# Scale columns by a product with ones, shift sums queued behind the scale sums, and transposes four steps later

## The chip, the cores and the metric

The kernel runs on one core of a Trainium2 chip. A core has a tensor engine (TensorE, PE in the profile; PEld is its loading of weights), a vector engine (VectorE, DVE), a scalar engine (ScalarE, ACT), GpSimd (POOL) and SyncE (SP), on which most transfers are issued. Each engine works through its own list of instructions in a fixed order and waits where an operand or a buffer isn't ready. The metric is the device time of one execution in microseconds (us), the median of several runs.

## The reference

One layer of a hybrid decoder block on a sequence of S = 512 tokens with D = 2048 channels, all in float32. A vector c sets six modulation vectors; the first norm's output is scaled by one and shifted by another; one wide input projection (7168 columns) feeds eight heads of dilated window attention and eight heads of a gated linear recurrence (HGRN2); then an output projection, a second modulated norm and a squared-ReLU MLP. What matters for this change is the head of it:

```
mod = silu(c) @ w_ada + b_ada                    # 2048 -> 6 * 2048
shift1, scale1, gate1, shift2, scale2, gate2 = split(mod, 6)
h = rms_norm(x, norm1_w) * (1 + scale1) + shift1
proj = h @ w_in                                  # 512 x 2048 by 2048 x 7168
aq, ak, av, gq, gf, gi, gg = split(proj)         # gq at 3072, gf at 4096, gi at 5120
```

## The kernel before

**Splitting.** A float32 product is made from three products of rounded parts: a matrix is cast to a high part (`whi`, `hi`; ScalarE) and VectorE subtracts it to get the low part (`wlo`, `lo`); hi·hi, hi·lo and lo·hi are summed. A weight block of 128 x 512 so costs one ScalarE cast (L39), one VectorE subtraction (L40) and three times as many matmuls. The pool `wr` keeps four blocks of each kind, so a new `whi` waits until TensorE has read the one four before it.

**Scale and shift as sums on VectorE.** A product of a vector with a matrix is done by `gemv` (L113 to L131): rows of the matrix come by DMA into `araw`, and VectorE adds, row group by row group, `araw * vec[k]` into two sums `acc` (L127 the first two, L129 the others). What remains is a sum over the 128 partitions. `to_cols` (L138 to L152) does it: four TensorE transposes of 128 x 128 (L149), then ScalarE copies with an accumulated row sum (L152), which leaves the result as a column per 128 channels. `mod_cols` (L160 to L170) adds the bias (L167) and, for the scale, forms `(1 + scale) * norm weight` (L169), both on VectorE. The scale is made in eight blocks of 256 columns, each enough for two channel tiles; the shift in four blocks of 512.

**First stage, scale only.** `x` is normalised and transposed to sixteen tiles `xnT` (128 channels x 512 tokens). `first_groups(4096, 3072, ...)` then runs over the sixteen channel tiles k, in pairs: `scale_block(k0)` makes the scale block of that pair and calls `scaled(k)`: ScalarE multiplies `xnT` by the column `g1c` (L332), casts it to `hi` (L333), and VectorE forms `lo` (L334). Per k there are 18 matmuls of 128 x 512 (L206 to L208): twelve for gf's first 512 columns (banks `prj`) and six for gq's first 256 (`prc`). The shift is left out here and added to the results afterwards.

**Second stage.** After k0 = 14, `shift_start` starts the shift: `bgw` is a list of generators, and every `bg_step()` runs one of them to its next `yield`. The same loops run again for the next columns with `shift_block` after each pair; once a shift block is done, `shifted(k)` adds the column `s1c` to `xnT` and renews `hi` and `lo` (L337 to L339). 

**Third stage.** `shift_through(col0)` gives the contribution of the shift to the first stage's columns: a `gemv` with `s1c` over w_in's columns (16 steps), `to_cols` (1 step later the transposes), then the gates (`forget`) or the SiLU (L748 to L751). One for columns 4096 and one for 3072 run during the end of the second stage and during `hv0`, the projection of gi (columns 5120), which has twelve matmuls per k (L198 to L200) and makes two background steps per k. What is left of `bgw` after `hv0` is run at once by `while bgw: bg_step()`, ahead of `q0`, the next projection. Then come k, v, the recurrence, the attention, the output projection and the MLP.

**What sets the order.** Through the second stage a scheduler orders each engine's list by estimated times; `tc.issue_after(x)` forbids an instruction ahead of x. From `hv0` on, TensorE's list follows the order in which the code is written, while the other engines' lists are still ordered by the scheduler.

Of the kernel before, what the change touches and what calls it, by code (L numbers as in the profile page):

```python
# [44 lines left out]
def hybrid_block(ctx, tc, x, c, positions, norm1_w, w_ada, b_ada, w_in, q_norm_w, k_norm_w,  # L45
# [3 lines left out]
    pe, dve, act, pool = nc.tensor, nc.vector, nc.scalar, nc.gpsimd  # L49
# [3 lines left out]
    ada_v = w_ada[0].rearrange("(k p) n -> p k n", p=P)  # L53
# [14 lines left out]
    def bank(name, tag="bg"):  # L68
        return ps.tile([P, 512], F32, name=name, tag=tag)


    ident = const.tile([P, P], F32, name="ident")
    make_identity(nc, ident)
    mhalf = const.tile([P, 32], F32, name="mhalf")
    pool.memset(mhalf, -0.5)

    crow = ca.tile([P, P], F32, name="crow", tag="rows")
    nc.sync.dma_start(crow[0:NK], c[0].rearrange("(r p) -> r p", p=P))
# [4 lines left out]
    n1c = const.tile([P, NK], F32, name="n1c")  # L83
    dve.tensor_copy(n1c, ps_c[:, NK:2 * NK])
    bcol = const.tile([P, 96], F32, name="bcol")
    dve.tensor_copy(bcol, ps_c[:, 2 * NK:P])
    sc = const.tile([P, NK], F32, name="sc")
    sig_ready = act.activation(sc, ps_c[:, 0:NK], AF.Sigmoid)
    sc_ready = dve.tensor_tensor(sc, ps_c[:, 0:NK], sc, op=ALU.mult)
# [26 lines left out]
    def gemv(view, vec, col0, n=512, early=False):  # L116

        accs = [(work("acc") if early else gv.tile([P, 512], F32, name="acc"))[:, 0:n] for _ in range(2)]
        nk = 512 // n
        for k0 in range(0, NK, nk):  # L120
            raw = spare.pop(0) if early and spare else slot("araw") if early else gv.tile([P, 512], F32, name="araw", bufs=4)
            raw = raw.rearrange("p (k n) -> p k n", n=n)
            nc.sync.dma_start(raw, view[:, k0:k0 + nk, col0:col0 + n])
            for k in range(k0, k0 + nk):
                acc = accs[k % 2]
                if k < 2:
                    dve.tensor_scalar(acc, raw[:, k - k0], vec[:, k:k + 1], None, op0=ALU.mult)  # L127
                else:
                    dve.scalar_tensor_tensor(acc, raw[:, k - k0], vec[:, k:k + 1], acc, op0=ALU.mult, op1=ALU.add)  # L129
            yield  # L130
        gemv.acc = accs  # L131

    def run_all(g):
        for _ in g:
            pass
        return gemv.acc

    def to_cols(accs, dst):  # L138

        nb = accs[0].shape[1] // P  # L140
        parts = 1 if nb == 4 else 2
        if parts == 1:
            dve.tensor_tensor(accs[0], accs[0], accs[1], op=ALU.add)
        yield
        pc = bank("pc")
        for j in range(nb):
            for u in range(parts):
                c = (j * parts + u) * P
                pe.transpose(pc[:, c:c + P], accs[u][:, j * P:(j + 1) * P], ident)  # L149
        for j in range(nb):  # L150
            c = pc[:, j * parts * P:(j + 1) * parts * P]
            act.activation(c, c, AF.Copy, accum_out=dst[:, j:j + 1])  # L152

    g1c = const.tile([P, NK], F32, name="g1c")
    s1c = const.tile([P, NK], F32, name="s1c")
# [1 line left out]
    s2c = const.tile([P, NK], F32, name="s2c")  # L157
    gcol = const.tile([P, NK], F32, name="gcol")

    def mod_cols(kind, b, dst, nw, n=512, early=False):  # L160

        for _ in gemv(ada_v, sc, kind * D + b * n, n, early):
            yield
        nb = n // P
        d = dst[:, b * nb:(b + 1) * nb]
        yield from to_cols(gemv.acc, d)
        dve.tensor_tensor(d, d, bcol[:, kind * NK + b * nb:kind * NK + (b + 1) * nb], op=ALU.add)  # L167
        if nw is not None:
            mod_cols.last = dve.scalar_tensor_tensor(d, d, 1.0, nw[:, b * nb:(b + 1) * nb], op0=ALU.add, op1=ALU.mult)  # L169
        yield  # L170

    def mod_rows(kind, dst):
# [53 lines left out]
    def slot(name, dt=F32):  # L226
        return io.tile([P, 512], dt, name=name, tag="io")

    def work(name, dt=F32):
        return wk.tile([P, 512], dt, name=name, tag="wk")  # L230

    def pair(i):

        return [hp.tile([P, S], F32R, name=f"{c}{i}", tag=f"{c}{i}") for c in ("hi", "lo")]
# [7 lines left out]
    hhi, hlo, spare = [], [], []  # L242


    first_scale = mod_cols(1, 0, g1c, n1c, 256, True)
    for _ in range(8):
        next(first_scale)
    xs = [[slot("xs") for _ in range(4)] for _ in range(NT)]
# [5 lines left out]
    for q in range(4):  # L254
        for ti in range(NT):
            jk = work("jk")
            with tc.issue_after(sc_ready.ins), tc.issue_after(sig_ready.ins):
                if q == 3 and ti % 2:
                    dve.tensor_tensor_reduce(jk, xs[ti][q], xs[ti][q], op0=ALU.mult, op1=ALU.add, scale=1.0, scalar=0.0,
                                             accum_out=ssx[:, ti, q:q + 1])  # L260
# [2 lines left out]
    dve.tensor_reduce(rx, ssx, axis=AX.X, op=ALU.add)  # L263
    rstd_of(rx, rx, NT, 1.0 / D)
    run_all(first_scale)
    second_scale = mod_cols(1, 1, g1c, n1c, 256, True)
    spare.extend(hp.tile([P, 512], F32, name="araw", tag=f"{c}{k}") for k in range(8, NK) for c in ("hi", "lo"))
    for _ in range(8):
        next(second_scale)
    xnT = []  # L270
# [29 lines left out]
    def scale_block(k0):  # L300
        if k0 == 0:
            run_all(second_scale)
        elif k0 < 14:
            run_all(mod_cols(1, k0 // 2 + 1, g1c, n1c, 256, True))
        for k in (k0, k0 + 1):
            scaled(k)

    def shift_start(k0):
        if k0 == 14:
            for _ in range(12):  # L310
                bg_step()

    shift_done, behind = set(), []

    def shift_gen(b):
        yield from mod_cols(0, b, s1c, None, 512, True)
        shift_done.add(b)

    def shift_block(k0):
# [9 lines left out]
    def scaled(k):  # L329
        for l, t in zip((hhi, hlo), pair(k)):  # L330
            l.append(t)
        act.activation(xnT[k], xnT[k], AF.Copy, scale=g1c[:, k:k + 1])  # L332
        act.copy(hhi[k], xnT[k])  # L333
        dve.tensor_tensor(hlo[k], xnT[k], hhi[k].bitcast(F32), op=ALU.subtract)  # L334

    def shifted(k):
# [404 lines left out]
    def shift_through(col0):  # L741

        yield from gemv(win_v, s1c, col0, early=col0 < 4096 + 512)
        col = sm.tile([P, 8], F32, name="scol", bufs=2)
        yield from to_cols(gemv.acc, col[:, 0:4])
        for h in range(4):
            if col0 == 3072:
                dve.tensor_scalar(col[:, 4 + h:5 + h], col[:, h:h + 1], QS, None, op0=ALU.mult)  # L748
                sg = wk.tile([P, 512], F32, name="sg", tag="ev", bufs=2)
                act.activation(sg, hq0[h], AF.Sigmoid, scale=1.0 / QS, bias=col[:, h:h + 1])  # L750
                dve.scalar_tensor_tensor(hq0[h], hq0[h], col[:, 4 + h:5 + h], sg, op0=ALU.add, op1=ALU.mult)  # L751
            else:
# [5 lines left out]
    bt, bc = first_groups(4096, 3072, scale_block, shift_start)  # L758
    f0 = keep(bt, "f")
    hq0 = keep(bc, "gq", QS)  # L760
    with tc.issue_after(mod_cols.last.ins):
        posf = ca.tile([NT, P], F32, name="posf")
        dve.tensor_copy(posf, posi)
        ps_v = bank("ps_v")
# [615 lines left out]
```

## Time and profile before

| | |
|---|---|
| median of 3 runs | 2312.09 us (2311.49 to 2312.19) |
| profiled execution | 2306.17 us |
| its span, first to last instruction | 2304.4 us |
| TensorE busy | 2230.5 us (97 %) |
| VectorE busy | 1825.9 us (79 %) |
| ScalarE busy | 1103.0 us (48 %) |
| mean granted TensorE clock | 0.994 |

Busy time is the union of an engine's instructions; matmuls overlap in the records, one of 128 x 512 lasting about 0.39 us and the next starting 0.227 us behind it. In the timeline a row stands for a run of like instructions, and a number in brackets at its end is the time in which the engine stood idle ahead of it, with the instruction that released it. Numbers behind names of buffers are left out in the profile; in the engines' lists below they are kept, since each `acc` there is one sum.

### The profile page before, as it was taken

To read this page: it belongs to the slowest core of one execution; us is meant where nothing else is said; L and a number is where in the kernel's file an instruction comes from. 1 tells how busy PE (TensorE), PEld (TensorE's weight loads), DVE (VectorE), ACT (ScalarE), POOL (GpSimd) and SP (SyncE) were. 2 spreads that over 40 slices of the span, in tenths; PEclk is the share of its full clock that TensorE was granted. 3 is DMA by queue.
4 is the path that set the end of the run, shared out by engine and by line. 5 is a ranking of instruction groups with operands and counts; after the bars stand their busy time and mean duration, and the time that the engine had idled before them with its cause. 6 is when DMAs were issued, how large, how long until landed. Compare 5 with 4: busy or idle time off the path is not lost.

```text
span 2304.4 us, 33163 instructions
## 1 busy us (share of the span) xinstructions
PE 2230.5 (97%) x11769; PEld 1829.2 (79%) x11769; DVE 1825.9 (79%) x2773; ACT 1103.0 (48%) x1958; POOL 458.1 (20%) x668
## 2 busy tenths in 40 slices
PE   4999999999999999999999999999998999999999
PEld 3787877888778888888887888888887888888887
DVE  6899777677776565669767988988895789967878
ACT  5555434433344553457644555565563333344332
POOL 1000022000230000001332323323232222222221
PEclk9999999999999999999999999999999999999999
DMA  9798455556545256746999799889889987999784
GB/s 327 249 337 314 123 176 156 176 162 215 178 149 182 74 186 218 259 132 220 366 382 382 252 341 355 301 297 380 310 295 369 339 288 262 364 336 335 277 302 165
DMA packets 264695, 606.71 MB, mean 263 GB/s; under 512 B 23284, under 2 KB 44032, under 8 KB 264528
## 3 DMA queue, kind: packets, MB, share of 16 engines
q1 hardware_dynamic: 186800, 332.54, 42.8%
q0 software_dynamic: 72832, 262.60, 31.1%
q10 hardware_dynamic: 4896, 9.44, 1.2%
q8 instruction: 93, 1.52, 0.3%
q14 instruction: 74, 0.61, 0.1%
HBM read 522.68 MB, written 81.81 MB: 262 GB/s over the span
## 4 chain that ended last, share of the span: by engine, by line
PE 56%; DMA 16%; DVE 14%; issue 10%; POOL 2%; ACT 1%; SPq 0%; DVEq 0%; POOLq 0%; ACTq 0%
PE f L1160 9%; PE f L1161 9%; PE f L1159 9%; DMA araw<-in_w_ada_dram 7%; PE prj L198 4%; PE prj L200 4%; PE prj L199 4%; DMA f_lod<-fs 3%; DVE acc L129 3%; PE f L208 2%; PE f L206 2%; PE f L207 2%; DVE vlo L1146 2%; DVE wlo L40 2%; PE prj L206 2%
## 5 line engine op out<-in xcount | busy, mean ns | idle before, releaser
L1145 ACT CAST vhi<-raw 128x1024 fp32r<-128x1024 f32 x392 | 412.8, 1055 | 547.1 <-PE f L1161 434.3
L1146 DVE TENSOR_TENSOR vlo<-raw,vhi 128x1024 fp32r<-128x1024 f32 x392 | 477.4, 1225 | 154.3 <-ACT vhi L1145 153.5
L1159 PE MATMUL f<-vhi,Fh 128*128 128x512 f32 x1376 | 537.6, 391 | 8.3 <-DMA Fh<-h_hid 3.6
L1160 PE MATMUL f<-vlo,Fh 128*128 128x512 f32 x1376 | 538.1, 391 | 3.0 <-DVE vlo L1146 3.0
L1161 PE MATMUL f<-vhi,Fl 128*128 128x512 f32 x1376 | 537.2, 390 | 2.1 <-DMA Fl<-f_lod 1.3
L39 ACT CAST whi<-wraw 128x512 fp32r<-128x512 f32 (+1 forms) x368 | 219.8, 601 | 449.3 <-PE prj L200 323.7
L198 PE MATMUL prj<-whi,hi 128*128 128x512 f32 x896 | 365.0, 407 | 1.3 <-ACT gg L698 1.3
L200 PE MATMUL prj<-whi,lo 128*128 128x512 f32 x896 | 351.5, 392 | 0.0
L199 PE MATMUL prj<-wlo,hi 128*128 128x512 f32 x896 | 350.8, 391 | 0.0
L40 DVE TENSOR_TENSOR wlo<-wraw,whi 128x512 fp32r<-128x512 f32 (+1 forms) x368 | 245.1, 670 | 111.7 <-ACT whi L39 107.1
L129 DVE SCALAR_TENSOR_TENSOR acc<-araw,sc,acc 128x512 f32<-128x512 f32 (+1 forms) x392 | 253.9, 678 | 98.5 <-DMA araw<-in_w_ada_dram 97.2
L1159 PEld LDWEIGHTS f<-vhi,Fh 128*128 128x128 f32 x1376 | 259.0, 188 | 63.3 <-issue 7.1
L1160 PEld LDWEIGHTS f<-vlo,Fh 128*128 128x128 f32 x1376 | 259.0, 188 | 61.7 <-DVE vlo L1146 8.3
L1161 PEld LDWEIGHTS f<-vhi,Fl 128*128 128x128 f32 x1376 | 259.1, 188 | 56.7 <-DMA Fl<-f_lod 1.8
L1129 DVE TENSOR_TENSOR raw<-raw,raw 128x1024 f32<-128x1024 f32 x224 | 269.5, 1223 | 1.8 <-DMA raw<-in_w_ff_dram 1.5
L198 PEld LDWEIGHTS prj<-whi,hi 128*128 128x128 f32 x896 | 169.4, 189 | 36.5 <-ACT gg L698 1.6
L200 PEld LDWEIGHTS prj<-whi,lo 128*128 128x128 f32 x896 | 168.9, 188 | 36.8
L199 PEld LDWEIGHTS prj<-wlo,hi 128*128 128x128 f32 x896 | 169.6, 189 | 32.4 <-DVE wlo L40 0.4
L1097 POOL DMA_DIRECT2D Fh<-f_hid x112 | 80.9, 722 | 428.3 <-PE f L1161 414.8
L208 PE MATMUL f<-hi,wlo 128*128 128x512 f32 x256 | 99.8, 390 | 0.6 <-DVE wlo L40 0.6
L206 PE MATMUL f<-hi,whi 128*128 128x512 f32 x256 | 100.2, 391 | 0.0
L207 PE MATMUL f<-lo,whi 128*128 128x512 f32 x256 | 99.6, 389 | 0.0
(306 smaller groups left out, 2956.9 us busy)
## 6 DMA issues: line engine op xcount, KB each, us to landing
raw<-in_w_ff_dram SPq DMA_DIRECT2D x224, 512.0 KB, 10.0
araw<-in_w_ada_dram SPq DMA_DIRECT2D x384, 256.0 KB, 4.3
Fh<-f_hid POOLq DMA_DIRECT2D x112, 512.0 KB, 6.5
Fl<-f_lod POOLq DMA_DIRECT2D x112, 512.0 KB, 7.4
wraw<-in_w_in_dram SPq DMA_DIRECT2D x104, 512.0 KB, 4.1
Fh<-h_hid POOLq DMA_DIRECT2D x60, 512.0 KB, 6.8
Fl<-h_lod POOLq DMA_DIRECT2D x60, 512.0 KB, 8.3
f_hid<-part POOLq DMA_DIRECT2D x48, 512.0 KB, 8.1
```

The lines of the kernel that those rows point to most:

```text
L39: nc.scalar.copy(hi, src)
L40: (eng or nc.vector).tensor_tensor(lo, src, hi.bitcast(F32), op=ALU.subtract)
L129: dve.scalar_tensor_tensor(acc, raw[:, k - k0], vec[:, k:k + 1], acc, op0=ALU.mult, op1=ALU.add)
L198: pe.matmul(banks[ti], lhsT=hi[:, ts], rhs=whi, start=first, stop=False)
L199: pe.matmul(banks[ti], lhsT=hi[:, ts], rhs=wlo, start=False, stop=False)
L200: pe.matmul(banks[ti], lhsT=lo[:, ts], rhs=whi, start=False, stop=last)
L1129: dve.tensor_tensor(dst, a, b, op=ALU.subtract)
L1145: act.copy(hi, src)
L1146: split_done.append(dve.tensor_tensor(lo, src, hi.bitcast(F32), op=ALU.subtract))
L1159: pe.matmul(banks[t], lhsT=fh[u][:, a, ts], rhs=whi[:, a], start=first, stop=False)
L1160: pe.matmul(banks[t], lhsT=fh[u][:, a, ts], rhs=wlo[:, a], start=False, stop=False)
L1161: pe.matmul(banks[t], lhsT=fl[u][:, a, ts], rhs=whi[:, a], start=False, stop=end)
```

## The change

There are five edits.

1. Scale blocks get a function of their own, `scale_cols`. The sum over partitions is a float32 product of the sum's 128 x 128 part (as weights) with a column of ones, four products per block in place of four transposes; the two sums `acc` are added in PSUM. ScalarE then forms the scale column from it in one instruction per column, with norm weight as scale and `(1 + bias) * norm weight` as bias (`b1c`, made once at the start); L152 and the two VectorE instructions L167 and L169 go for these blocks.
2. `scaled(k)` writes `hi` from `xnT` and `g1c` directly, ahead of the scaling of `xnT`.
3. The first twelve background steps, the start of the shift's sums, are held behind the last VectorE instruction of the last scale block; the tables for the rotary embedding behind that too.
4. `to_cols` gets a parameter `lag`, the number of background steps between the last sum and its transposes; `shift_through` passes 5 in place of 1.
5. `to_cols` and `mod_cols` lose the 256-column case.

```diff
+    pool.memset(mhalf[:, 16:32], 1.0)
+    ones = mhalf[:, 16:17]
...
+    b1c = bcol[:, NK:2 * NK]
+    dve.scalar_tensor_tensor(b1c, b1c, 1.0, n1c, op0=ALU.add, op1=ALU.mult)
...
+    def to_cols(accs, dst, lag=1):
+
+        dve.tensor_tensor(accs[0], accs[0], accs[1], op=ALU.add)
+        for _ in range(lag):
+            yield
         pc = bank("pc")
...
+    def scale_cols(b):
+
+        for _ in gemv(ada_v, sc, D + b * 256, 256, True):
             yield
+        accs = gemv.acc
+        scale_cols.last_dve = gemv.last
+        pc = bank("pc")
+        for j in range(2):
+            for u in range(2):
+                pe.matmul(pc[:, j:j + 1], lhsT=accs[u][:, j * P:(j + 1) * P], rhs=ones, start=u == 0, stop=u == 1)
+        for j in range(2):
+            ks = slice(2 * b + j, 2 * b + j + 1)
+            scale_cols.last = act.activation(g1c[:, ks], pc[:, j:j + 1], AF.Identity, scale=n1c[:, ks],
+                                             bias=b1c[:, ks])
+        yield
...
         if k0 == 14:
-            for _ in range(12):
-                bg_step()
+            with tc.issue_after(scale_cols.last_dve.ins):
+                for _ in range(12):
+                    bg_step()
...
+        act.activation(hhi[k], xnT[k], AF.Copy, scale=g1c[:, k:k + 1])
         act.activation(xnT[k], xnT[k], AF.Copy, scale=g1c[:, k:k + 1])
-        act.copy(hhi[k], xnT[k])
...
-        yield from to_cols(gemv.acc, col[:, 0:4])
+        yield from to_cols(gemv.acc, col[:, 0:4], 5)
...
-    with tc.issue_after(mod_cols.last.ins):
+    with tc.issue_after(scale_cols.last.ins), tc.issue_after(scale_cols.last_dve.ins):
```

VectorE's list near the end of the first stage, before: `acc_967` and `acc_968` are the sums of the scale block for k = 12 and 13, `acc_1076` and `acc_1077` those of the last block, `acc_1251` and `acc_1252` the first shift block; `g1c` is the scale column.

```order
L127 TENSOR_SCALAR acc_1251<-araw_1253,sc_86 128x512
L129 SCALAR_TENSOR_TENSOR acc_967<-araw_997,sc_86,acc_967 128x256
L129 SCALAR_TENSOR_TENSOR acc_1076<-araw_1090,sc_86,acc_1076 128x256
L127 TENSOR_SCALAR acc_1252<-araw_1256,sc_86 128x512
L167 TENSOR_TENSOR g1c_111<-g1c_111,bcol_84 128x2
L129 SCALAR_TENSOR_TENSOR acc_1077<-araw_1090,sc_86,acc_1077 128x256
L129 SCALAR_TENSOR_TENSOR acc_968<-araw_997,sc_86,acc_968 128x256
L40 TENSOR_TENSOR wlo_1027<-wraw_1020,whi_1026 128x512
L40 TENSOR_TENSOR wlo_1033<-wraw_1030,whi_1032 128x256
L129 SCALAR_TENSOR_TENSOR acc_1251<-araw_1259,sc_86,acc_1251 128x512
L129 SCALAR_TENSOR_TENSOR acc_1076<-araw_1094,sc_86,acc_1076 128x256
L129 SCALAR_TENSOR_TENSOR acc_1252<-araw_1262,sc_86,acc_1252 128x512
```

The same place now, where `acc_1064` and `acc_1065` are the last scale block and `acc_1237` and `acc_1238` the first shift block:

```order
L40 TENSOR_TENSOR wlo_1025<-wraw_1018,whi_1024 128x256
L133 SCALAR_TENSOR_TENSOR acc_1064<-araw_1086,sc_88,acc_1064 128x256
L133 SCALAR_TENSOR_TENSOR acc_1065<-araw_1086,sc_88,acc_1065 128x256
L133 SCALAR_TENSOR_TENSOR acc_1064<-araw_1090,sc_88,acc_1064 128x256
L133 SCALAR_TENSOR_TENSOR acc_1065<-araw_1090,sc_88,acc_1065 128x256
L133 SCALAR_TENSOR_TENSOR acc_1064<-araw_1094,sc_88,acc_1064 128x256
L133 SCALAR_TENSOR_TENSOR acc_1065<-araw_1094,sc_88,acc_1065 128x256
L131 TENSOR_SCALAR acc_1237<-araw_1239,sc_88 128x512
L131 TENSOR_SCALAR acc_1238<-araw_1242,sc_88 128x512
L782 CAST posf_1287<-posi_93 4x128
L353 TENSOR_TENSOR lo12_1106<-xnT_429,hi12_1105 128x512
```

The shift's sums have moved from among the scale's to behind their end, and the two small instructions on `g1c` (L167, and L169 a row later) are gone.

TensorE's list in `hv0`, at the transposes of the first `shift_through`: before,

```order
L200 MATMUL prj_2103<-whi_2244,lo6_793 128x512
L149 MATMUL pc_2266<-ident_69,acc_2058 128x128 x4
L198 MATMUL prj_2100<-whi_2248,hi7_797 128x512
L199 MATMUL prj_2100<-wlo_2249,hi7_797 128x512
L200 MATMUL prj_2100<-whi_2248,lo7_798 128x512
```

and now:

```order
L218 MATMUL prj_2089<-whi_2266,lo8_892 128x512
L151 MATMUL pc_2286<-ident_69,acc_2044 128x128 x4
L216 MATMUL prj_2086<-whi_2270,hi9_896 128x512
L217 MATMUL prj_2086<-wlo_2271,hi9_896 128x512
L218 MATMUL prj_2086<-whi_2270,lo9_897 128x512
```

They have moved from ahead of k = 7 to ahead of k = 9, past 24 matmuls.

VectorE's list at the border of `hv0` and `q0`, before: `acc_2295` is the sum of the second `shift_through` (columns 3072), `wlo_2448` the last low part of `hv0`, and `wlo_2523` to `wlo_2622` the first four of `q0`.

```order
L40 TENSOR_TENSOR wlo_2444<-wraw_2441,whi_2443 128x512
L129 SCALAR_TENSOR_TENSOR acc_2984<-araw_3120,sc_86,acc_2984 128x512
L143 TENSOR_TENSOR acc_2295<-acc_2295,acc_2296 128x512
L40 TENSOR_TENSOR wlo_2448<-wraw_2441,whi_2447 128x512
L40 TENSOR_TENSOR wlo_2523<-wraw_2520,whi_2522 128x512
L40 TENSOR_TENSOR wlo_2527<-wraw_2520,whi_2526 128x512
L40 TENSOR_TENSOR wlo_2618<-wraw_2615,whi_2617 128x512
L40 TENSOR_TENSOR wlo_2622<-wraw_2615,whi_2621 128x512
```

Now, with `acc_2315` for the same sum, `wlo_2422` the last low part of `hv0` and `wlo_2509` to `wlo_2608` the first four of `q0`:

```order
L40 TENSOR_TENSOR wlo_2422<-wraw_2415,whi_2421 128x512
L40 TENSOR_TENSOR wlo_2509<-wraw_2506,whi_2508 128x512
L40 TENSOR_TENSOR wlo_2513<-wraw_2506,whi_2512 128x512
L40 TENSOR_TENSOR wlo_2604<-wraw_2601,whi_2603 128x512
L40 TENSOR_TENSOR wlo_2608<-wraw_2601,whi_2607 128x512
L133 SCALAR_TENSOR_TENSOR acc_2315<-araw_2469,s1c_114,acc_2315 128x512
L133 SCALAR_TENSOR_TENSOR acc_2316<-araw_2472,s1c_114,acc_2316 128x512
L145 TENSOR_TENSOR acc_2315<-acc_2315,acc_2316 128x512
```

The sum over the two halves has moved from ahead of `hv0`'s last low part to behind the fourth low part of `q0`. On TensorE the transposes of this sum stand in both kernels between the last matmul of `hv0` and the first of `q0`; before, `bgw` is empty when `hv0`'s sixteen k are done, and now the eight steps that the two lags add are left for `while bgw`.

## Rows read from the trace of the kernel before

**Rows 1.** Waits of TensorE: line, what released it, total us, times, longest.

```profile
PE prj L206 <- ACT hi L333: 6.9, 4, 4.1
PE pc L149 <- DVE acc L143: 4.9, 1, 4.9
PE pC L645 <- DVE z L598: 4.2, 2, 3.1
```

**Rows 2.** Busy time by stretch, PE to POOL, then TensorE's clock, DMA share, GB/s.

```profile
80.00:100.00 20.00, 15.65 (x60) 11.73 (x59) 20.00 (x48) 9.09 (x21) 0.00 (x0) 0.84 0.77 262
100.00:120.00 20.00, 20.00 (x90) 16.26 (x89) 13.56 (x46) 10.10 (x21) 0.00 (x0) 0.98 0.29 80
120.00:190.00 70.00, 69.99 (x315) 57.43 (x314) 67.20 (x127) 41.55 (x94) 4.75 (x8) 1.00 0.97 346
```

**Rows 3.** VectorE's timeline, 90 to 93 us: start, length, instructions.

```profile
90.64 1.82 DVE L129 SCALAR_TENSOR_TENSOR acc<-araw,sc,acc 128x512 f32<-128x512 f32 x3
92.36 0.17 DVE L169 SCALAR_TENSOR_TENSOR g1c<-g1c,n1c 128x2 f32<-128x2 f32 x1
```

**Rows 4.** ScalarE's timeline, 86 to 95 us.

```profile
86.63 0.20 ACT L152 ACTIVATION_READ_ACCUMULATOR pc<-pc 128x1 f32 x1
...
92.57 1.33 ACT L332 ACTIVATE xnT<-xnT,g1c 128x512 f32<-128x512 f32 x2 [1.14 <-DVE g1c L169]
```

**Rows 5.** TensorE's timeline, two waits of the first stage and the matmuls behind them.

```profile
52.75 2.02 PE L206 MATMUL prj<-hi,whi 128*128 128x512 f32 x4 [1.97 <-ACT hi L333]
...
56.27 0.40 PE L207 MATMUL prj<-lo,whi 128*128 128x512 f32 x1
...
94.46 2.07 PE L206 MATMUL prj<-hi,whi 128*128 128x512 f32 x4 [4.05 <-ACT hi L333]
...
100.74 0.39 PE L207 MATMUL prc<-lo,whi 128*128 128x512 f32 x1
```

**Rows 6.** TensorE's timeline, transposes of one scale block; float32 products of the recurrence.

```profile
46.97 0.60 PE L149 MATMUL pc<-ident,acc 128*128 128x128 f32 x4
47.33 0.48 PE L206 MATMUL prc<-hi,whi 128*128 128x512 f32 x1
...
279.37 0.38 PE L678 MATMUL pho<-gi,AT 128*128 128x128 f32 x2
279.59 0.39 PE L678 MATMUL pho<-gi,far_sb 128*128 128x128 f32 x2
```

**Rows 7.** Groups of one line: durations ns (least, median, most), first and last start, forms.

```profile
L662 PE MATMUL pD<-z x32: 270/275/377, 272.1 to 681.8; 128*128 128x128 f32 x32
L88 ACT ACTIVATE sc<-ps_c x1: 183/183/183, 5.8 to 5.8; 128x16 f32<-128x16 f32 x1
```

**Rows 8.** SyncE's queue: loads of w_in from 90.47, their length, then shift loads.

```profile
90.47 30.29 SPq L189 DMA_DIRECT2D wraw<-in_w_in_dram  x7
```

**Rows 9.** DMA issues of the page: KB each, us from issue to landing.

```profile
araw<-in_w_ada_dram SPq DMA_DIRECT2D x384, 256.0 KB, 4.3
```

**Rows 10.** VectorE's timeline: the 13th background step's sums, in `hv0`, at `q0`.

```profile
126.37 3.05 DVE L129 SCALAR_TENSOR_TENSOR acc<-araw,sc,acc 128x512 f32<-128x512 f32 x4
...
214.24 0.69 DVE L143 TENSOR_TENSOR acc<-acc 128x512 f32<-128x512 f32 x1
...
229.64 1.42 DVE L129 SCALAR_TENSOR_TENSOR acc<-araw,s1c,acc 128x512 f32<-128x512 f32 x2
...
243.71 0.69 DVE L40 TENSOR_TENSOR wlo<-wraw,whi 128x512 fp32r<-128x512 f32 x1 [2.51 <-ACT whi L39]
```

**Rows 11.** TensorE's timeline in `hv0`, then at its end.

```profile
214.98 1.12 PE L149 MATMUL pc<-ident,acc 128*128 128x128 f32 x4 [4.86 <-DVE acc L143]
...
220.14 0.39 PE L199 MATMUL prj<-wlo,hi 128*128 128x512 f32 x1
...
242.38 0.60 PE L149 MATMUL pc<-ident,acc 128*128 128x128 f32 x4
```

**Rows 12.** ScalarE's timeline at the end of `hv0`.

```profile
243.06 0.62 ACT L39 CAST whi<-wraw 128x512 fp32r<-128x512 f32 x1
```

More of the change, by code (lines that the diff above doesn't have):

```diff
@@ L74, in hybrid_block @@
     mhalf = const.tile([P, 32], F32, name="mhalf")
-    pool.memset(mhalf, -0.5)
+    pool.memset(mhalf[:, 0:16], -0.5)
+    pool.memset(mhalf[:, 16:32], 1.0)
+    ones = mhalf[:, 16:17]
     crow = ca.tile([P, P], F32, name="crow", tag="rows")
@@ L128, in gemv @@
                 else:
-                    dve.scalar_tensor_tensor(acc, raw[:, k - k0], vec[:, k:k + 1], acc, op0=ALU.mult, op1=ALU.add)
+                    gemv.last = dve.scalar_tensor_tensor(acc, raw[:, k - k0], vec[:, k:k + 1], acc, op0=ALU.mult,
+                                                         op1=ALU.add)
             yield
@@ L136, in run_all @@
         return gemv.acc
[L138 to L144, printed above, removed]
-        pc = bank("pc")
[L146 to L152, printed above, removed]
+    def to_cols(accs, dst, lag=1):
+        dve.tensor_tensor(accs[0], accs[0], accs[1], op=ALU.add)
+        for _ in range(lag):
+            yield
+        pc = bank("pc")
+        for j in range(4):
+            js = slice(j * P, (j + 1) * P)
+            pe.transpose(pc[:, js], accs[0][:, js], ident)
+        for j in range(4):
+            js = slice(j * P, (j + 1) * P)
+            act.activation(pc[:, js], pc[:, js], AF.Copy, accum_out=dst[:, j:j + 1])
     g1c = const.tile([P, NK], F32, name="g1c")
@@ L158, in hybrid_block, with mod_cols @@
     gcol = const.tile([P, NK], F32, name="gcol")
-    def mod_cols(kind, b, dst, nw, n=512, early=False):
-        for _ in gemv(ada_v, sc, kind * D + b * n, n, early):
+    def scale_cols(b):
+        for _ in gemv(ada_v, sc, D + b * 256, 256, True):
             yield
-        nb = n // P
+        accs = gemv.acc
[9 more added lines that the diff above has]
+        yield
+    def mod_cols(kind, b, dst, nw, early=False):
+        for _ in gemv(ada_v, sc, kind * D + b * 512, 512, early):
+            yield
+        nb = 4
         d = dst[:, b * nb:(b + 1) * nb]
@@ L168, in mod_cols @@
         if nw is not None:
-            mod_cols.last = dve.scalar_tensor_tensor(d, d, 1.0, nw[:, b * nb:(b + 1) * nb], op0=ALU.add, op1=ALU.mult)
+            dve.scalar_tensor_tensor(d, d, 1.0, nw[:, b * nb:(b + 1) * nb], op0=ALU.add, op1=ALU.mult)
         yield
@@ L242, in hybrid_block @@
     hhi, hlo, spare = [], [], []
-    first_scale = mod_cols(1, 0, g1c, n1c, 256, True)
+    first_scale = scale_cols(0)
     for _ in range(8):
@@ L265, in hybrid_block @@
     run_all(first_scale)
-    second_scale = mod_cols(1, 1, g1c, n1c, 256, True)
+    second_scale = scale_cols(1)
     spare.extend(hp.tile([P, 512], F32, name="araw", tag=f"{c}{k}") for k in range(8, NK) for c in ("hi", "lo"))
@@ L303, in scale_block @@
         elif k0 < 14:
-            run_all(mod_cols(1, k0 // 2 + 1, g1c, n1c, 256, True))
+            run_all(scale_cols(k0 // 2 + 1))
         for k in (k0, k0 + 1):
@@ L309, in shift_start @@
         if k0 == 14:
-            for _ in range(12):
-                bg_step()
+            with tc.issue_after(scale_cols.last_dve.ins):
+                for _ in range(12):
+                    bg_step()
     shift_done, behind = set(), []
     def shift_gen(b):
-        yield from mod_cols(0, b, s1c, None, 512, True)
+        yield from mod_cols(0, b, s1c, None, True)
         shift_done.add(b)
```

## The prediction

> **What bounds the kernel now.** I read the busy shares first: TensorE works 97 % of the span, so the change can win only where TensorE waits. Next the waits of TensorE, grouped [rows 1]: two groups belong to lines that the change touches, 6.9 us on `hi` (L333) in four waits and 4.9 us on a VectorE sum (L143) in one. Then the busy time by stretch [rows 2]: from 80 to 100 us VectorE has no free moment, TensorE works 15.65 of 20 us and its granted clock is 0.84, so some of that time was at the lower of its two levels (1.2 against 2.4 GHz). From 100 to 120 VectorE works only 13.56 of 20, and from 120 to 190 again 67.2 of 70. Last the timelines of four engines around the waits.
>
> The wait of 4.05 us shows how the loss comes about. ScalarE has finished the column sums of that scale block at 86.83 (86.63 + 0.20) [rows 4], but the scale column is ready only at 92.53, because L169 stands on VectorE behind low parts and three other sums, two of them the shift's, which nobody needs yet [rows 3]. ScalarE then scales two tiles before it casts, and TensorE starts at 94.46 [rows 5]. The kernel pays for a 2-element instruction with a queue.
>
> A wait costs more than its length. From 52.75 to 56.27 stand 8 matmuls, which at the usual spacing of some 0.227 us (315 in 70 us, a few of them short [rows 2]) take 1.8 us: 1.7 lost behind a gap of 1.97. From 94.46 to 100.74 stand 14, worth 3.2: 3.1 lost behind 4.05 [rows 5]. From 214.98 to 220.14 stand four transposes (0.36 [rows 6]) and ten matmuls (2.27): 2.5 lost behind 4.86 [rows 11].
>
> **First stage.** L167 and L169 leave VectorE and with them the queue between sum and column. In their place ScalarE makes two columns itself; its nearest row is an activation of 128x16 in 0.18 us [rows 7]. `hi` comes first, 0.67 us (half of 1.33 for two scalings [rows 4]). So for the block above `hi` would be there some 0.4 + 0.7 us, and with the products below 2 us, behind the sums, at about 87 to 88, while TensorE is free for it at 90.41 (94.46 - 4.05). The scale sums themselves keep up: VectorE no longer does the first twelve shift sums (two at the front, ten at 0.71 [rows 10], about 7.5 us) ahead of the last ones, which end some 8 us earlier. The waits of 1.97 and 4.05 go, and of the two small ones behind `hi` (0.9 together) half: 6.4. With them goes the loss at the low clock, 1.7 + 3.1 = 4.8.
>
> The four products cost more than the four transposes. Four transposes take 0.36 (47.33 - 46.97). A float32 product of 128 columns is two records 0.11 apart: 0.22 for two records [rows 6], 32 records for 16 products in the program [rows 7]. Four products are then eight records, 0.88, so 0.5 more per block; seven of the eight blocks lie in the dense part: 3.6 us. Here one column moves and not 128. The ends: nothing extra, if a record with one column is half as long, and 6.3, if each product takes 0.32, as it would at the lower clock. I take 3.6, since the row is for the same weights. First stage: 6.4 + 4.8 - 3.6 = 7.6 us.
>
> A rule of the Trainium skill (FP8 and Floating Point Precision, TensorE Precision Notes) speaks against this edit: a true float32 product makes four passes through the array. The trace disagrees for this kernel's float32 products, with two records each [rows 7]. By the rule a block would cost 16 records, 1.76 us.
>
> **Second stage and `hv0`.** What is queued behind the moved sums? SyncE is held from 90.47 to 120.8 by loads of w_in, whose ring moves with TensorE, and the thirteenth and later shift loads stand behind them [rows 8]; VectorE adds the first of these at 126.37 [rows 10] and from there on is full [rows 2]. So that start comes earlier by what TensorE gained, 7.6, perhaps a little more, as VectorE's idle 6.4 us between 100 and 120 takes in the moved sums. From there to the first `shift_through`'s sum, VectorE's list is longer than before by two low parts and six sums, 0.60 and 0.67 each as they are spaced (their records, 0.69 and half of 1.42 [rows 10], overlap the next a little): 5.2. The sum ended at 214.93 [rows 10]; now 214.93 - 7.6 + 5.2 = 212.5. TensorE reached its transposes at 210.1 (214.98 - 4.86) and has 24 more matmuls (5.45) before them: 210.1 + 5.45 - 7.6 = 207.95. It is 4.5 us early, or 3.2 if the loads are added as soon as they land (4.3 us behind their issue [rows 9], where before they were added 5.6 behind the first issue: 126.37 - 120.8, so 1.3 earlier). The price of before, 4.86 + 2.5 = 7.4, becomes 3.2, taken in two pieces (the transposes of the fourth shift block stand 38 matmuls earlier than before and wait about half), and since short gaps lose less at the clock, 1.2 with them: 4.4. Gain 3.0. The ends: 7.4, if VectorE catches up, and -1, if 4.5 with a full clock loss stays.
>
> **The border of `hv0` and `q0`.** The eight steps that the lags add are left over there, and this is a new wait. Before, the second sum stood ahead of `hv0`'s last low part, and its transposes at 242.38 bear no mark of a wait [rows 11]. Now two sums and the final one stand behind `q0`'s fourth low part, whose `whi` needs the ring slot that `hv0`'s last matmul frees, and on ScalarE the copies of `hv0`'s results come before that `whi`. Before, this `whi` starts at 243.06 [rows 12] and the low part at 243.71 [rows 10]. So: 243.71 + 0.60 + 1.33 (two sums) + 0.60 = 246.2, against 242.38: TensorE waits 3.9 us, with the rest of `q0` queued behind its transposes. By the three gaps above the clock takes 1.7 to 3.1 more; I take 2.3. Cost 6.2. The ends: 0, if the sums overtake the low part's release, and 7.
>
> **Sum.** 7.6 + 3.0 - 6.2 = 4.4 us gained. Against the profiled execution, 2306.17, that is 2301.8; the median shown is 5.9 us above it, so 2312.1 - 4.4, about 2308. The one more instruction at the start (VectorE, 128x16) I cost at nothing: it lies beside the ScalarE activation of the same shape there [rows 7], and if that cover fails it costs about as much, 0.2.
>
> **The rivals.** (a) No wait at the border, and VectorE catches up in `hv0`: 7.6 + 4 to 7 - 0 to 2, about 2300. For it: VectorE idles up to 2.5 us at a time there [rows 10]. Against: its list is fixed, and the sum stands behind the low part in it. (b) VectorE is the bound from 120 us on, and what the first stage gains is only waited for in `hv0`: 7.6 - 1 - 6.2, or 2312. For it: 67.2 of 70 us. Against: loads that start earlier. (c) Slower: the late second sum makes the SiLU of gq late, with it the first level products of the recurrence, whose sums wait already (4.2 us on `z` [rows 1]); they share VectorE with `q0`'s low parts, which the left-over steps have pushed together. It would add 3 to 8 us to the 6.2, about 2316; it decides as soon as this second wait is over 4.4. Against it: TensorE's border wait delays TensorE and the chain alike. (d) The products take four passes: 1.4 more per block than transposes, 9.8 in place of 3.6, so the gain becomes a loss of 1.8: 2314. The rule above names it; the records of before are against it. That the shift's sums do not move is excluded by VectorE's list.
>
> **Numbers.** Forecast 42 %, (a) 18 %, (b) 20 %, (c) 13 %, (d) 7 %. What this kernel's measurements can tell from no change is about 0.2 %, 4.6 us. The forecast lies at that bound: half of it counts as faster (22 %, 19 % same, 1 % slower); (a) gives 17 % faster and 1 % same; (b) 2, 14 and 4; (c) 0, 2 and 11; (d) 0, 3 and 4. Together faster 41 %, same 39 %, slower 20 %. The range from 2298 to 2317 takes in (a) and most of (c); the forecast's own is 2303 to 2313.
>
> **What would show it.** Right: no waits on `hi` from 45 to 100 us, and the clock 1.00 there; eight records per block at the products, about 0.9 us; the shift's first sums behind the last scale sum; a wait of 2 to 4 us in `hv0` or at the fourth shift block; a wait of about 4 us on the sum's last addition between `hv0` and `q0`. Wrong: 16 records per block, waits on the products' sums in place of those on `hi`, or no wait at the border.

## The result, and the profile after

The changed kernel is slower: 2313.74 us (median of 20 runs, 2309.58 to 2321.71) against 2308.52 us (20 runs, 2301.07 to 2315.95), a ratio of 1.0024 with a 95 % interval of 1.0013 to 1.0034. The profiled execution has a span of 2310.7 us, against 2304.4. Forecast was 2308 and 4.4 us of gain, from the median of 2312.09 of three runs; of the twenty runs beside the changed kernel the median before is 2308.52, so the gain and not the 2308 is what can be compared. What came is a loss of 5 to 6 us.

The waits of TensorE over the whole span, changed kernel (line, what released it, total us, times, longest), which answer to [rows 1]:

```profile
PE pc L151 <- DVE acc L145: 6.8, 2, 4.0
PE pC L664 <- DVE z L617: 6.2, 4, 2.5
...
PE pB L590 <- DVE z L617: 2.5, 3, 1.0
PE pC L670 <- DVE z L617: 2.4, 3, 1.1
...
PE pD L681 <- DVE z L617: 1.8, 2, 1.3
PE prj L217 <- DVE wlo L40: 1.6, 2, 1.4
...
PE prj L224 <- ACT hi L351: 0.5, 1, 0.5
```

The 6.9 us on `hi` have become 0.5. But the sums (L145, before L143) now cost 6.8 in place of 4.9, in two waits, and the recurrence's products wait for `z` 13.6 us in five groups (the 0.7 of the smallest isn't shown), where before it was 7.6 in three (4.2, 2.9 and 0.5).

Busy time by stretch, changed kernel (PE, PEld, DVE, ACT, POOL, then clock, DMA share, GB/s), against [rows 2]:

```profile
80.00:100.00 20.00, 20.00 (x101) 16.88 (x100) 20.00 (x48) 11.26 (x24) 0.00 (x0) 1.00 0.76 265
120.00:190.00 70.00, 67.93 (x306) 55.46 (x305) 68.84 (x121) 41.30 (x98) 4.36 (x8) 1.00 0.96 339
...
235.00:255.00 20.00, 16.03 (x150) 12.43 (x150) 12.41 (x28) 7.59 (x19) 0.00 (x0) 0.83 0.25 80
535.00:710.00 175.00, 166.29 (x1566) 132.08 (x1565) 135.30 (x306) 68.29 (x228) 32.50 (x54) 1.00 0.56 176
```

The last stretch in the kernel before:

```profile
535.00:710.00 175.00, 171.88 (x1595) 136.88 (x1594) 138.22 (x311) 71.81 (x232) 37.54 (x54) 1.00 0.58 180
```

From 80 to 100 us TensorE is full and at full clock: the first stage does what was forecast. From 120 to 190, where it was full before (69.99), it now has gaps; from 235 to 255 it idles 4 us and the clock is 0.83; from 535 to 710 it idles 8.7 us, before 3.1.

Where the time goes is best read as a race between the two profiles. The table gives the start of ScalarE's copies of finished results in each: the first copy of `f` ends the first stage, the last copy of `gi` ends `hv0`, the last of `aq` ends `q0`, and the last of `av` in the second half ends v1.

| | before | after | after is earlier by |
|---|---|---|---|
| first stage's first result | 119.9 | 111.7 | 8.2 |
| second stage's last result | 191.2 | 185.5 | 5.7 |
| `hv0` | 242.6 | 235.9 | 6.7 |
| `q0` | 299.5 | 299.7 | -0.2 |
| v1 | 702.2 | 707.8 | -5.6 |
| span | 2304.4 | 2310.7 | -6.3 |

Three losses follow the gain: a small one in the second stage and `hv0`, one of 6.9 us within `q0`, and one of 5.4 us between `q0` and v1. TensorE's timeline, changed kernel, at the first two losses (start, length, in brackets the idle time ahead):

```profile
181.43 0.51 PE L216 MATMUL prj<-whi,hi 128*128 128x512 f32 x1 [1.03 <-ACT whi L39]
...
182.76 0.73 PE L226 MATMUL prc<-hi,wlo 128*128 128x512 f32 x2 [0.83 <-DVE wlo L40]
...
198.10 0.50 PE L217 MATMUL prj<-wlo,hi 128*128 128x512 f32 x1 [1.42 <-DVE wlo L40]
...
214.59 0.86 PE L151 MATMUL pc<-ident,acc 128*128 128x128 f32 x4 [2.83 <-DVE acc L145]
...
239.87 1.12 PE L151 MATMUL pc<-ident,acc 128*128 128x128 f32 x4 [3.97 <-DVE acc L145]
...
245.78 0.39 PE L216 MATMUL prj<-whi,hi 128*128 128x512 f32 x1
```

And VectorE's at the border of `hv0` and `q0`, against [rows 10]:

```profile
237.07 0.69 DVE L40 TENSOR_TENSOR wlo<-wraw,whi 128x512 fp32r<-128x512 f32 x1 [2.50 <-ACT whi L39]
237.68 1.41 DVE L133 SCALAR_TENSOR_TENSOR acc<-araw,s1c,acc 128x512 f32<-128x512 f32 x2
239.12 0.69 DVE L145 TENSOR_TENSOR acc<-acc 128x512 f32<-128x512 f32 x1
```

The border is as the prediction drew it: the low part that waits for `whi`, two sums, the last addition, and TensorE 3.97 us late. From 239.87 to 245.78 stand four transposes (0.36) and twelve matmuls (2.72), so the low clock takes 2.8 more.

### The profile page after: what moved, and what is told of

The parts are those of the page before. It is cut to its first block, busy times and chain, and to the rows that moved or that the text cites. A ratio compares the mean times of both kernels' runs of the same rounds, so it can differ in the third digit from the quotient of the medians.

```text
span 2310.7 us, 33190 instructions
## 1 busy us (share of the span) xinstructions
PE 2231.6 (97%) x11801; PEld 1831.6 (79%) x11801; DVE 1826.7 (79%) x2758; ACT 1102.5 (48%) x1942; POOL 455.0 (20%) x669
## 4 chain that ended last, share of the span: by engine, by line
PE 61%; DMA 11%; DVE 11%; issue 6%; POOL 1%; ACT 1%; SPq 0%; DVEq 0%; POOLq 0%; ACTq 0%
PE f L1180 11%; PE f L1179 11%; PE f L1178 10%; PE prj L216 5%; PE prj L218 5%; PE prj L217 5%; DMA araw<-in_w_ada_dram 5%; PE f L226 2%; PE f L225 2%; PE f L224 2%; DVE acc L133 2%; DMA Fl<-h_lod 2%; DMA f_lod<-fs 2%; DVE vlo L1165 2%; DVE wlo L40 1%
## 5 line engine op out<-in xcount | busy, mean ns | idle before, releaser
L40 DVE TENSOR_TENSOR wlo<-wraw,whi 128x512 fp32r<-128x512 f32 (+1 forms) x368 | 243.9, 667 | 117.3 <-ACT whi L39 115.5
```

The source lines that it names most:

```text
L40: (eng or nc.vector).tensor_tensor(lo, src, hi.bitcast(F32), op=ALU.subtract)
```

## The experiments

Each kernel was timed in turn with the kernel before on the same chip; the ratio is to that, with its 95 % interval. Waits and the end of `hv0` (before: 242.6) come from one profile each. "z waits" are TensorE's waits for `z` from 535 to 710 us.

| | ratio | interval | end of `hv0` | z waits |
|---|---|---|---|---|
| before | 1 | | 242.6 | 3.1 |
| changed kernel | 1.0024 | 1.0013 to 1.0034 | 235.9 | 8.7 |
| e1: lag 1 | 1.0023 | 1.0008 to 1.0037 | 240.8 | 5.6 |
| e2: 2.5 steps per k | 1.0024 | 1.0007 to 1.0042 | 237.8 | 8.1 |
| e3: lag alone | 1.0028 | 1.0012 to 1.0045 | 235.2 | 7.1 |
| e4: without the hold | 1.0011 | 0.9995 to 1.0028 | 230.4 | 8.8 |
| e5: columns alone | 0.9990 | 0.9977 to 1.0003 | 236.1 | 4.1 |
| e6: third lag 1 | 1.0002 | 0.9990 to 1.0014 | 237.0 | 5.1 |
| e7: columns, first lag 5 | 0.9965 | 0.9951 to 0.9980 | 233.3 | 4.9 |
| e8: hold alone | 0.9983 | 0.9971 to 0.9996 | 238.7 | 3.2 |
| e9: third lag alone | 1.0034 | 1.0022 to 1.0046 | 242.1 | 7.8 |
| e10: e7 with the hold | 1.0009 | 0.9995 to 1.0023 | 238.4 | 4.5 |
| e11: e7 with lag 9 | 0.9952 | 0.9938 to 0.9967 | 229.4 | 5.7 |
| e12: e9 with few loads | 0.9926 | 0.9901 to 0.9951 | 241.6 | 0 |

**e1, the changed kernel with lag 1.**

```diff
-        yield from to_cols(gemv.acc, col[:, 0:4], 5)
+        yield from to_cols(gemv.acc, col[:, 0:4], 1)
```

> The changed kernel with the lag of shift_through back to 1 (edit 4 undone alone). Theory A: the loss is made by the lag, by the left-over steps at the border of hv0 and q0 (a wait of 4.0 us and 3.4 us at the low clock) and by the shifted background steps in the recurrence (TensorE waits there 5 to 6 us longer from 535 to 710 us). Then no wait at the border, the wait in hv0 grows to about 8 us (2.8 plus 24 matmuls), and the kernel is 3 to 6 us faster than the one before. Rival B: the recurrence loses because TensorE arrives earlier than VectorE's list allows, whatever the lag: then the waits from 535 to 710 us stay at 8 us or more and the time is within 3 us of the changed kernel's.

The border wait is gone, `hv0` waits 7.7 us in one piece, as expected, and the z waits fall from 8.7 to 5.6. But the time does not follow: 1.0023, no faster than the changed kernel, where theory A had it 3 to 6 us faster than the one before. So the lag is not the only loss; something in the other edits costs too. `q0` still ends 1.8 us earlier than before (297.7 against 299.5), but from there to v1 this profile takes 408.2 us, as the changed kernel does (408.1) and not 402.7 as before, with the clock low near 380, 470 and 670 us. So rival B, that the recurrence loses whatever the lag, is refuted neither by the time nor by that stretch.

**e2, no steps left over.**

```diff
-    hv0 = evac(project(5120, tok_mm, 2.0), "gi")
+    hv0 = evac(project(5120, tok_mm, 2.5), "gi")
```

> The changed kernel with 2.5 in place of 2 background steps per k in hv0, so that none is left over at the border; the lag stays. Theory A in its narrow form (the border is what costs): the wait of 4.0 us there and the low clock behind it go, the transposes in hv0 come 12 matmuls earlier and wait 2 to 3 us more; 4 to 6 us faster than the changed kernel. If the shifted steps in the recurrence cost (the third shift_through has the lag too), the waits from 535 to 710 us stay at 8 us, and it is no faster than the one before. Rival B: as the changed kernel, less the 4 us at most.

No border wait, 5.5 us in `hv0`; `q0` ends at 294.7, 5.0 us ahead of the changed kernel. At v1 it is 0.6 us behind (708.4), with 8.1 us of z waits and three stretches of low clock on the way, and the ratio is the same. Taking the border away alone brings nothing that the time shows. This also speaks against the rival (c) of the prediction: without the late second sum the z waits are as long.

**e3, the kernel before with the lag alone.**

```diff
-        yield from to_cols(gemv.acc, col[:, 0:4])
+        yield from to_cols(gemv.acc, col[:, 0:4], 5)
```

> The kernel before with the lag of 5 alone. Theory A: the first stage keeps its two waits; the wait in hv0 (4.9 us) goes or shrinks, the border wait (4 us) comes, and the recurrence loses 5 us or more from 535 to 710 us: 4 to 8 us slower than before. Rival B: the recurrence is as before, 0 to 2 us slower in all.

1.0028, as theory A had it: edit 4 by itself costs about as much as the whole change (the intervals overlap). In `hv0` it does what it was for (7.4 us earlier, no wait), the border then takes most of that back (a wait of 4.6 us), and the z waits grow to 7.1.

**e4, no hold.**

```diff
-            with tc.issue_after(scale_cols.last_dve.ins):
-                for _ in range(12):
-                    bg_step()
+            for _ in range(12):
+                bg_step()
```

> The changed kernel without the hold of the first twelve background steps behind the last scale sum (edit 3 undone in part). Theory A: the first stage keeps 4 to 8 us of its gain, since the queue between sum and column is gone anyway, with small waits on the scale sums (1 to 3 us); VectorE is earlier with the shift, so the waits of 1 to 1.4 us on low parts from 180 to 200 us shrink; the border and the recurrence as in the changed kernel, so within 3 us of it. Rival C: the hold is what makes VectorE late from 180 us on: then the waits from 180 to 215 us, 6.3 us in the changed kernel, fall below 3 and the time falls by 3 us or more.

No wait from 120 to 230 us, and `hv0` ends 5.5 us earlier than with the hold, although the first stage's first result stands at 116.6 in place of 111.7. The border's wait stays: 4.3 us, up to 234.7. Rival C, that the hold makes VectorE late there, is supported by the waits; the time (1.0011) is too uncertain to tell from 1.0024.

**e5, the columns alone (edits 1 and 2).** The diff is that of e4 and of e1 together.

> Edits 1 and 2 alone (products with ones, hi first): no hold, lag 1. Theory A (each lag and the hold cost, the columns gain): the first stage keeps its gain (the stage's results leave hv0's start 4.5 us earlier than before, as without the hold), the wait in hv0 before k = 7 stays near 5 to 8 us, no border wait, recurrence as before (q0's end to v0 of the second half 402 to 404 us): 3 to 5 us faster than before. Rival B (arriving earlier costs later): no faster than before, the gain lost in the recurrence.

`hv0` waits 4.86 us again, exactly as before, but ends 6.5 us earlier; 0.9990. From `q0` to v1 it takes 402.9 us, as before. Right in kind, less in size than the 3 to 5 us expected (about 2, and no change isn't excluded).

**e6, lag 5 for two of the three.**

```diff
-        yield from to_cols(gemv.acc, col[:, 0:4], 5)
+        yield from to_cols(gemv.acc, col[:, 0:4], 1 if col0 == 4096 + 512 else 5)
```

> The changed kernel with the lag of 5 for the two shift_through that run in hv0, but 1 for the third (columns 4608), which runs during the recurrence. Theory A: the border wait of 4 us stays, but from q0's end to the second half's v0 it takes 402 to 404 us as before in place of 408: 4 to 6 us faster than the changed kernel. Rival B: that stretch stays at 407 or more, and the time with it.

1.0002: 0.0022 below the changed kernel, 5 us, by one number for a `shift_through` that the prediction didn't price. The stretch from `q0` to v1 took 408.4 us in this one profile, which has three stretches of low clock that the changed kernel's has not, so there the expectation is not met and rival B stands; the z waits are 5.1.

**e7, columns, no hold, the lag for columns 4096 alone.** On top of e4:

```diff
-        yield from to_cols(gemv.acc, col[:, 0:4], 5)
+        yield from to_cols(gemv.acc, col[:, 0:4], 5 if col0 == 4096 else 1)
...
-    hv0 = evac(project(5120, tok_mm, 2.0), "gi")
+    hv0 = evac(project(5120, tok_mm, 2.25), "gi")
```

> Edits 1 and 2, no hold, the lag of 5 only for the shift_through of columns 4096, and 2.25 background steps per k in hv0, so that none is left at the border. Theory A: first stage 4.5 us earlier, the wait in hv0 at most 2 us, no border wait, the recurrence as before: 9 to 12 us faster than before (ratio 0.995 to 0.996). Rival B: the recurrence takes 5 us of it, 3 to 6 us faster.

0.9965, 8 us faster than before: a little under the 9 to 12 of theory A. The wait in `hv0` is 2.13 us, the border has none.

**e8, the kernel before with the hold alone.**

```diff
-            for _ in range(12):
-                bg_step()
+            with tc.issue_after(mod_cols.last.ins):
+                for _ in range(12):
+                    bg_step()
```

> The kernel before with the hold of the first twelve background steps behind the last scale instruction on VectorE (edit 3 alone). Theory A: the wait of 4.05 us in the first stage shrinks by 1 to 2 us (two shift sums less in the queue), but VectorE starts the shift 7 us later and the waits from 180 to 230 us grow by about 5 us: 2 to 5 us slower than before. Rival C: the hold costs nothing, since VectorE's idle 6.4 us from 100 to 120 us take in the moved sums: within 2 us.

0.9983: faster, where theory A said slower and C within 2 us (the interval goes down to 0.9 us, so C isn't excluded). The longest wait of the first stage falls from 4.05 to 2.8 us (first row, waits from 36 to 120 us; the other two from 120 to 200):

```profile
PE prj L206 <- ACT hi L334: 5.9, 4, 2.8
...
PE prc L208 <- DVE wlo L40: 1.0, 1, 1.0
PE prj L199 <- DVE wlo L40: 0.8, 1, 0.8
```

The low clock behind it goes too: the first stage's first result stands at 114.5, 5.4 us earlier. The new waits on low parts in the second stage are there, but cost less than that.

**e9, the kernel before with the third lag alone.**

```diff
-        yield from to_cols(gemv.acc, col[:, 0:4])
+        yield from to_cols(gemv.acc, col[:, 0:4], 5 if col0 == 4096 + 512 else 1)
```

> The kernel before with the lag of 5 for the third shift_through (columns 4608) alone; everything up to q0 stays as before. Theory A (this lag is what costs in the recurrence): up to q0's end the same times as before, then the waits on z from 535 to 710 us grow from 3 to 7 us or more, and the kernel is 3 to 6 us slower than before (ratio 1.0015 to 1.0025). Rival B (the recurrence loses because TensorE or VectorE come to it in another state, not through this lag): within 2 us of before.

1.0034, more than the 1.0015 to 1.0025 expected, from a change that begins behind `hv0`. In the profile, 6.2 us longer than that of before, 3.4 are lost between `q0` and v1 (406.1 against 402.7) and 3.2 behind v1; that all of the timed loss arises in the recurrence is not shown. The z waits are 7.8. Where they come from is seen at the longest. TensorE's timeline of e9:

```profile
677.74 0.45 PE L646 MATMUL pC<-z 128*32 128x32 f32 x16 [2.85 <-DVE z L599]
```

VectorE's ahead of it, e9:

```profile
671.95 0.42 DVE L605 TENSOR_TENSOR Sx<-Sx,f 128x256 f32<-128x256 f32 x1
674.70 0.75 DVE L129 SCALAR_TENSOR_TENSOR acc<-araw,sc,acc 128x512 f32<-128x512 f32 x1 [2.34 <-DMA araw<-in_w_ada_dram]
675.37 0.42 DVE L615 TENSOR_TENSOR mt<-mt 128x256 f32<-128x256 f32 x1
...
677.18 0.42 DVE L599 TENSOR_TENSOR z<-gq,f 128x256 f32<-128x256 f32 x1
```

A background sum stands in VectorE's list between two steps of the recurrence and waits 2.34 us for its load; everything behind it, `z` at the end, waits with it. In the kernel before, the same steps (L604, then L614 to L598) follow one another, and the sum that waits for its load stands ahead of them:

```profile
668.48 0.75 DVE L129 SCALAR_TENSOR_TENSOR acc<-araw,sc,acc 128x512 f32<-128x512 f32 x1 [2.74 <-DMA araw<-in_w_ada_dram]
...
671.82 0.42 DVE L604 TENSOR_TENSOR Sx<-Sx,f 128x256 f32<-128x256 f32 x1
672.15 0.42 DVE L614 TENSOR_TENSOR mt<-mt 128x256 f32<-128x256 f32 x1
```

It costs TensorE a wait of 1.81 us there, at 671.36. e9 has such a wait too (1.73 us at 671.49) and the 2.85 us on top of it. The changed kernel has the pattern of e9, VectorE and then TensorE:

```profile
677.30 0.75 DVE L133 SCALAR_TENSOR_TENSOR acc<-araw,sc,acc 128x512 f32<-128x512 f32 x1 [2.01 <-DMA araw<-in_w_ada_dram]
```

```profile
680.35 0.45 PE L664 MATMUL pC<-z 128*32 128x32 f32 x16 [2.52 <-DVE z L617]
```

**e10, e7 with the hold.** The diff of e7 on the changed kernel.

> The best version so far (edits 1 and 2, lag 5 for columns 4096 alone, 2.25 background steps per k) with the hold put back. Theory D (columns and hold cure the same wait, and what the hold adds in the first stage is taken back because VectorE sets the end of the second stage): the first stage's results 4 us earlier than without the hold, but waits on low and high parts from 180 to 200 us and a wait of 4 us or more in hv0, so hv0 ends 3 to 5 us later and the kernel is 3 to 6 us slower than without the hold. Rival C: the hold is harmless, as it was alone: within 2 us of the version without it.

1.0009 against 0.9965 without: the hold costs 0.4 % here, about 10 us, more than the 3 to 6 of theory D. Up to `hv0` theory D is met: the first stage's first result stands 4.0 us earlier (111.5 against 115.5), there are waits of 2.2 us on parts from 120 to 200 us and one of 5.5 us in `hv0` (last row, from 200 to 250; e7 has 2.1 there), and `hv0` ends 5.1 us later.

```profile
PE prj L216 <- ACT whi L39: 1.0, 1, 1.0
PE prc L226 <- DVE wlo L40: 0.8, 1, 0.8
PE prj L217 <- DVE wlo L40: 0.4, 1, 0.4
...
PE pc L151 <- DVE acc L145: 5.5, 1, 5.5
```

The transposes that wait for that sum, in e7 and then in e10:

```profile
209.24 0.66 PE L151 MATMUL pc<-ident,acc 128*128 128x128 f32 x4 [2.13 <-DVE acc L145]
```

```profile
214.58 1.12 PE L151 MATMUL pc<-ident,acc 128*128 128x128 f32 x4 [5.50 <-DVE acc L145]
```

With the hold the sum is ready 5.3 us later.

**e11, a lag of 9 and 2.5 steps per k.** On e7:

```diff
-        yield from to_cols(gemv.acc, col[:, 0:4], 5 if col0 == 4096 else 1)
+        yield from to_cols(gemv.acc, col[:, 0:4], 9 if col0 == 4096 else 1)
...
-    hv0 = evac(project(5120, tok_mm, 2.25), "gi")
+    hv0 = evac(project(5120, tok_mm, 2.5), "gi")
```

> The same version without the hold, with a lag of 9 for columns 4096 and 2.5 background steps per k: the transposes stand 12 matmuls (2.7 us) later. The wait of 2.1 us in hv0 and the low clock behind it (1.7 us) go; theory: 2 to 4 us faster than with the lag of 5, hv0's end at 230 us. Rival: VectorE gets more sums ahead of that one by the higher rate, and the time stays within 1 us.

`hv0` has no wait and ends at 229.4, 3.9 us earlier. 0.9952, the fastest version of all, 11 us under the kernel before; against e7 the intervals overlap, so the 2 to 4 us expected over e7 are not shown. From 210 to 220 us, where the kernel before stood half idle, TensorE is full and at full clock:

```profile
210.00:220.00 10.00, 10.00 (x47) 8.28 (x46) 9.91 (x18) 7.24 (x17) 0.00 (x0) 1.00 0.85 291
```

**e12, e9 with few loads.**

```diff
+        ring, held = [], view is ada_v
...
+            if early or not held or k0 < 4:
...
+                ring.append(raw)
+            else:
+                raw = ring[k0 % 4]
```

> The kernel before with the lag of 5 for the third shift_through alone, and in addition the background sums over w_ada from hv0 on load only their first four row groups and use them again for the other twelve (the modulation values from there on are left out of the computation in this sense; the number of VectorE instructions stays). TensorE's list is unchanged. Theory A (a background sum that waits for its load stands on VectorE ahead of the recurrence's products z, and the lag moves the sums to such places): the waits on z from 535 to 710 us, 7.8 us with the loads, fall below 3 us, and so do those from 250 to 420 us (4.1). Rival E (the sums' own 0.66 us each ahead of z, with or without their loads): the waits stay at 6 us or more from 535 to 710 us. The time itself also falls because fewer bytes are moved, so it is read from the waits.

TensorE's busy time from 535 to 710 us, e12:

```profile
535.00:710.00 175.00, 175.00 (x1550) 139.75 (x1549) 144.90 (x325) 73.11 (x241) 33.86 (x54) 1.00 0.35 102
```

and e9:

```profile
535.00:710.00 175.00, 167.06 (x1573) 132.73 (x1572) 137.31 (x307) 69.68 (x230) 34.34 (x54) 1.00 0.56 175
```

With most of the loads gone, and VectorE's sums still there (it works more in the stretch, not less), TensorE does not wait once, and VectorE's waits for these loads fall from 21.5 to 3.6 us. That fits theory A. But VectorE's list is not that of e9: the scheduler has ordered it anew, and at the place of e9's longest wait no sum stands between the steps:

```profile
661.62 0.41 DVE L610 TENSOR_TENSOR Sx<-Sx,f 128x256 f32<-128x256 f32 x1
661.95 0.42 DVE L620 TENSOR_TENSOR mt<-mt 128x256 f32<-128x256 f32 x1
```

So e12 does not separate the wait for the load from the place of the sum. That the load is the larger part is read from e9's rows: at 674.70 VectorE idles 2.34 us for it, and the sum itself takes some 0.67. The 4.1 us from 250 to 420 fell to 2.1, below the 3 expected, but not to nothing, so there part of the waits has another cause.

## Why the prediction was wrong

**First stage: right.** 7.6 us were forecast, 8.2 came. The two waits went with their low clock, and the products cost what their records said. TensorE's timeline, changed kernel, the last scale block:

```profile
97.54 0.95 PE L171 MATMUL pc<-mhalf,acc 128*128 128x1 f32 x8
98.35 0.49 PE L224 MATMUL prj<-hi,whi 128*128 128x512 f32 x1
```

Eight records for four products and 0.81 us, against the 0.88 of [rows 6] and 128 columns: one column is hardly cheaper. That rules out the price of rival (d), 16 records and 1.76 us. It doesn't tell the number of passes, for which the prediction took the records: as one column takes almost as long as 128, neither the count of the records nor their time says how often the columns went through, and "the trace disagrees" said too much. The sum didn't hang on it. The 0.32 us per product, from which the term's upper end was made, stands in no row.

**Second stage and `hv0`: mis-sized.** I took 3.0 us of further gain there; it was a loss of 1.5 (8.2 to 6.7). The wait on the sum was 2.83 and 1.7 at the clock, near the 4.4 priced, but that is luck: TensorE came to it at 211.8 and not at 207.95, and the sum was ready at 214.5 and not at 212.5. (The lower end of this term, -1, doesn't come out of its own numbers either: 7.4 less 4.5 less at most 3.1 is -0.2.) What I left out are waits on parts between 180 and 200 us, 3.5 us together: 1.03 for a `whi` of ScalarE, which works without a break behind the last shift column of VectorE (from 173.8 us), and 0.83, 0.20 and 1.42 for VectorE's `wlo`. I had VectorE start earlier with TensorE and saw that it was full, but asked only for the sum in `hv0`, not for each low part on the way. The runs tie these waits to the hold: the changed kernel, e1, e2, e6, e8 and e10 have the hold and waits on parts there; e3, e4, e5, e7, e9 and e11 have neither. In all versions with the columns or the hold, the second stage ends between 185.0 and 187.2 us. With the hold TensorE waits for parts on the way, so their making sets the end; in e4, e5, e7 and e11, without it, TensorE has no wait from 120 to 200 us and sets the end itself. What the hold adds to the columns' gain in the first stage is gone by then, and the sum of the first `shift_through` comes later: the transposes stand at 214.58 in e10 against 209.24 in e7, and at 213.73 in e1 against 208.65 in e5. Columns and hold cure the same wait. Alone the hold helps (0.9983) and the columns perhaps (0.9990); both without the lag do not (e1, 1.0023). Why the two together end slower than before, and not merely no faster, no run settles: e1 is still 1.8 us ahead at the end of `q0` and loses it behind. The hold with the first lag but without the columns was not run either.

**Border: right.** 6.2 us were forecast; 3.97 of wait and 2.8 at the clock came, 6.8.

**The recurrence: the step that failed.** The sum gave edit 4 a place in `hv0` and at the border only. But `shift_through` has a third caller, columns 4608, whose steps run during the recurrence, and by its lag all background sums behind it stand four steps later in the program. I put this at nothing and read VectorE's list to the border and no further. e9 isolates that lag on the kernel before: 1.0034, as much as the whole loss. e6 takes it out of the changed kernel: 1.0002 in place of 1.0024, 5 us. How it costs is seen in the rows of e9 and of the changed kernel: a background sum that waits for its load comes to stand between the steps that make `z`. e12 fits that, but its list differs in order too. And the lag is not all of it: with the third lag at 1, the versions with the columns have z waits of 4.1 to 5.7 us, against 3.1 before, and e1 and e6 take as long from `q0` to v1 as the changed kernel; this part stays open. My rival (c) had the right place, and its 3 to 8 us take in the 5.4, but the wrong cause, the late second sum: in e2 that sum isn't late and the z waits are 8.1 us, and in e9 nothing before the recurrence is changed.

So: 8.2 gained, 1.5 lost to VectorE, 6.9 at the border, 5.4 from there to v1, 0.7 later. That makes 10.7 us against the forecast, of which the recurrence is 5.4 and `hv0` 4.5. The 0.7 is less than profiles differ by: from v1 to the end e1 to e11 take between 1599.7 and 1611.3 us.

## What to carry to other kernels

When a helper gets a parameter, price it at every caller, and follow each engine's list to the end of the work that it moves. Where an engine works through its list in a fixed order, an instruction that waits for a load belongs where nothing urgent stands behind it: in e9 the place of such a sum cost more than its length. And two cures for one wait don't add up; here the second one moved work to where VectorE was full already, and without it the kernel was 0.4 % faster (e7 against e10).

## What the hardware showed that I had not expected

TensorE's low clock also came where its waits are short. Behind the 2.83 us at 214.59 the clock took 1.7 us, and behind the 3.12 us wait of the kernel before at 387 us about as much. e7, with a wait of 2.13 us in `hv0`, has a granted clock of 0.84 from 210 to 220 us. Behind about 1 us it came or didn't: in the changed kernel the clock stayed at 1.00 behind the waits of 1.03 us at 181 us and of 1.42 us at 198 us, while in e1, e2, e6 and e10, with waits of 1.02 to 1.21 us at the first of these places, it was 0.83 from 180 to 190 us. Single profiles differ by some us for that alone; so a comparison of ends rests on the timed runs, and the profile only says where to look.
